# A decoder layer in fp32: one more pair of the down product in its 7-product form, four preparatory jobs moved ahead to the z products, a sixth pair's forms kept in device memory

## The chip, the cores and the metric

The kernel runs on one core of one Trainium2 chip. The metric is the device time of one execution in microseconds, the median of the runs. Before the change it is 992.4 us (three runs, 992.35 to 993.69).

## What is computed

One layer of a hybrid decoder: 256 tokens, 2048 features, float32. Cut to what matters here:

```python
h = rms_norm(x, g_mix)
z = h @ w_in                       # pool | q latent | kv latent | rope key | memory query
y = concat(pool_mixer(z_pool), mla(z_q, z_kv, z_kr), mem_attention(z_mq, mem))
x = x + y @ w_o
h = rms_norm(x, g_ffn)
g = causal_conv3(h @ w_gate) + conv_b
x = x + (silu(g) * (h @ w_up)) @ w_down      # 5632 hidden features
```

The change touches the last product, `@ w_down`, and when preparations for it are made.

## The kernel before, in words

**Arithmetic.** Every large product is made in three matmuls of a reduced float32 type: each operand is split into a high part (a rounding copy) and a low part (the rest), and high x high, low x high and high x low are added up in PSUM. For a weight tile, `split_w` has ScalarE write the high part `wh` (L102) and VectorE the low part `wl` (L103); there are four buffers of each, so the splits run at most four tiles of 128x1024 ahead of TensorE.

**Stages in order of time.** Memory keys and values (`mg`, until about 50 us); memory query and rope key (until 76.8); the z products, `gemm_z` (L140), six for the q and kv latents and one for the pool, with the memory attention between them (until about 126); pool, q and kv products with the rest of the attention preparation; output product `w_o` with the attention heads beside it; gate and up products, 44 steps f of two 1 MB weight tiles each (from about 302 to 770 us); down (770 to 987 us).

**Down.** The 5632 hidden features are 22 pairs of 128-wide blocks. A pair with the two halves of the tokens and the two 512-wide parts of 1024 columns makes a 2x2 block product. A plain pair (`plain`, L961) does its 8 block products, 3 matmuls each: 24 matmuls of 128x512. A pair in the 7-product form (`seven`, L990) does 7 products of sums of blocks (a Strassen-Winograd scheme): 21 matmuls. This needs sums of the activations' blocks, the "forms" `aS` (made in `glu` when the pair's gate and up steps are done, L892 to L900: 14 blocks of 128x128, 896 KB), and sums of the weight blocks (four subtractions of 128x512 on VectorE). Down runs over two halves c of the columns, and in each over the 22 pairs in the order `ORDER`. `KIND` gives the kind of each place in that order:

- p: plain; the pair's weight tile (1024 KB) is loaded and split;
- S: 7-product, with weight sums made earlier by a "job" and kept in device memory (`tsum`); in down three blocks of the weight tile (768 KB) and the tile of sums (1024 KB) are loaded;
- s: 7-product, with sums made in down by VectorE (`make_sums`, L982), which runs between the splits of the pair ahead.

Loads of down go out on SP's queue into six tiles in rotation (three `wr`, two `wj`, one in `dn`). Pairs in `AWAY` don't fit into SBUF: their forms are stored to device memory after `glu` (L902) and fetched again in each half into the one buffer `aL` (`fetch`, L975, on POOL's queue). The first fetch of a half is issued at its start, each further one right behind the pair that used the buffer (L1056).

**Jobs.** A job loads a weight tile of down (`job_load`, POOL's queue), makes its four sums in place on VectorE (`job_sums`, L760 to L766) and stores them to `tsum` in two pieces, again from POOL. Before, there are 30 jobs: eight during the output product (`first_jobs`), 22 during the gate and up products.

**What sets the order.** The code is recorded step by step; a scheduler may shift steps on an engine, except those marked `keep`, which stay in program order among themselves. Each engine then runs its list in order, and a DMA is issued when its queue reaches it and its waits are met. Job loads, job sums and stores are kept. The four buffers `wh` and `wl` and the load tiles are released by their last reader.

**Around the z products.** Three `wr` tiles hold the weights; SP loads them as they come free, with two loads of x rows (`x1n`, L538) among them. After the memory query, `mq_done` (L441) has ScalarE copy the results, TensorE transpose them and ScalarE write `mqT` (L282), which the memory scores (L511) use between the second z product's low and high parts.

Of the kernel before, what the change touches and what calls it, by code (L numbers as in the profile page):

```python
# [11 lines left out]
F32 = mybir.dt.float32  # L12
# [3 lines left out]
ALU = mybir.AluOpType  # L16
AX = mybir.AxisListType

P = 128
# [13 lines left out]
KF = DFF // P  # L33
# [3 lines left out]
STG = 2048  # L37
HS = 1024
NN = 512

PAIRS = KF // 2
KIND = "pSSSsSSpSSsSSSSsSSSSpp"
ORDER = (0, 1, 16, 2, 3, 4, 17, 5, 21, 6, 18, 7, 8, 9, 19, 10, 11, 12, 20, 13, 14, 15)
AWAY = (16, 17, 18, 19, 20)
SEVEN = tuple(j for j, k in zip(ORDER, KIND) if k != "p")
SUMMED = tuple((c, j) for c in range(2) for j, k in zip(ORDER, KIND) if k == "S")

# [17 lines left out]
def layer(ctx, tc, xT_d, xn_d, memT_d, vec_d, tab_d, w_z_d, w_mqkr_d, w_q_d, w_kv_d, w_mem_d, w_pool_d, w_o_d,  # L65
          w_g_d, w_u_d, w_dn_d, out_d):
    nc = tc.nc
# [8 lines left out]
    def nm(s):  # L76
        uid[0] += 1
        return f"{s}_{uid[0]}"

    def ps_main():  # L80
        return psm.tile([P, 512], F32, tag="m", name=nm("psm"))
# [4 lines left out]
    def load_w(src, n, cut=STG, kept=False):  # L86
        raw = stage.tile([P, STG], F32, tag="wr", name=nm("wr"), bufs=3)
        for c in range(0, n, cut):
            keep(nc.sync.dma_start(raw[:, c:min(n, c + cut)], src[:, c:min(n, c + cut)]), kept)
        return raw[:]  # L90

    def keep(ins, on=True):

        return tc.keep_in_program_order(ins) if on else ins
# [93 lines left out]
    def split_act(dst, src, scale=None, kept=False):  # L188


        h, l = (dst[:, 0], dst[:, 1]) if len(dst.shape) == 3 else (dst[:, 0:T], dst[:, T:2 * T])
        if scale is None:
            nc.scalar.copy(h, src)
            nc.vector.tensor_tensor(l, src, h.bitcast(F32), op=ALU.subtract)
        else:
            keep(nc.scalar.activation(h, src, AF.Copy, scale=scale), kept)
            keep(nc.vector.scalar_tensor_tensor(l, src, scale, h.bitcast(F32), op0=ALU.mult, op1=ALU.subtract), kept)
# [4 lines left out]
    def v(name, i=0):  # L202
        o = VOFF[name] + i
        return vec[:, o:o + 1]
# [9 lines left out]
    big = ctx.enter_context(tc.tile_pool(name="big", bufs=1))  # L214
    mix = ExitStack()
    mp = mix.enter_context(tc.tile_pool(name="mix", bufs=1))
# [18 lines left out]
    def tok():  # L235
        return mp.tile([P, 512], F32, tag="tok", name=nm("tok"), bufs=3)
# [105 lines left out]
    for c in range(KD // 2):  # L342
        raw = raw0 if c == 0 else load_w(w_mem_d[c], STG, HS if c == 1 else STG)
# [9 lines left out]
        if c % 2:  # L353
            h = slice(2 * c - 2, 2 * c + 2)
# [68 lines left out]
    for c in range(KD // 2):  # L423
        raw = load_w(w_mqkr_d[c], 2 * 576)
# [97 lines left out]
    def mem_steps(m):  # L522
        if m == 0:
            mq_done()
        for h, step in beside.get(m, ()):
            (mem_heads[h].score, mem_heads[h].turn, mem_heads[h].values)[step]()
        if m == 6:
            latent_scales()

    zl = mp.tile([P, 6, 2 * T], F32R, tag="zl", name="zl")  # L530
    zs = mp.tile([P, 2, T], F32, name="zs")

# [2 lines left out]
    for m in range(6):  # L535
        raw = load_w(w_z_d[m], STG)
        if m in (1, 3):
            keep(nc.sync.dma_start(x1n[:, m // 2, :], xn_d[m // 2]))  # L538
        ps = ps_main()[:, 0:T]
        gemm_z(ps, raw, xg, lambda: mem_steps(m), m % 2 == 1)  # L540
        a = zs[:, m // 4, :]
        if m % 4 == 0:
            nc.scalar.activation(a, ps, AF.Square)
        else:
            t = mp.tile([P, T], F32, tag="zsq", name=nm("zsq"), bufs=2)
            nc.scalar.activation(t[:], ps, AF.Square)
            nc.vector.tensor_tensor(a, a, t[:], op=ALU.add)
        split_act(zl[:, m, :], ps, v("g_q_lat", m) if m < 4 else v("g_kv_lat", m - 4))


    sl, sl2 = sm(4), sm(4)

    def latent_scales():
        ps = ps_aux()
        for i in range(2):
            col_sums(ps[:, 2 * i:2 * i + 2], zs[:, i, :])
        for i in range(2):
            o = slice(2 * i, 2 * i + 2)
            nc.vector.tensor_tensor(sl[:, o], ps[:, o], rx2, op=ALU.mult)
            rsqrt_(sl[:, o], sl[:, o], 1.0 / (QR if i == 0 else KVR))  # L560
            nc.vector.tensor_tensor(sl[:, o], sl[:, o], rx, op=ALU.mult)
        nc.vector.tensor_tensor(sl2, sl, sl, op=ALU.mult)
# [6 lines left out]
    def pool_in(g):  # L569
        raw = load_w(w_z_d[6 + g], STG)  # L570
        ps = ps_main()[:, 0:T]
        gemm_z(ps, raw, xg, lambda: mem_steps(6 + g), False) if g == 0 else gemm_t(ps, raw, 0, xg, range(KD))
        nc.vector.tensor_tensor(zp[:, g, :], ps, rxb[:], op=ALU.mult)
# [46 lines left out]
    def q_up(n):  # L620
        raw = load_w(w_q_d[n], STG)
        pss = [[ps_main()[:]] for _ in range(NT)]
        for i in range(2):
            hi, lo = split_w(raw, i * HS, HS)
            gemm_n(pss, hi.rearrange("p (k n) -> p k n", n=512), lo.rearrange("p (k n) -> p k n", n=512),
                   zl, 2 * i, i == 0, i == 1)
        for tt in range(NT):
            ps = pss[tt][0]
            t = tok()
            if n < 2:  # L630
                nc.scalar.copy(t[:], ps)
                head_sq(ssq_n[:, tt, 4 * n:4 * n + 4], t[:].rearrange("p (h d) -> p h d", d=NOPE))
                to_features(qnT[:, 4 * n:4 * n + 4], t, tt, 4, gqk[:, 0:1])
            else:
                t1 = tok()
                nc.scalar.copy(t1[:], ps)
                p3 = t1[:].rearrange("p (h d) -> p h d", d=ROPE)
                head_sq(ssq_r[:, tt, :], p3)
                rotate(t[:].rearrange("p (h d) -> p h d", d=ROPE), p3, 0, tt, H)
                to_features(qrT, t, tt, 4)  # L640
# [34 lines left out]


    pool_in(0)
    q_up(2)
    pool_in(1)
    kv_up(0)  # L680
# [65 lines left out]
        if done[0] == 4 * H + 4:  # L746
            mla_heads[H - 1].values()

    dp = ctx.enter_context(tc.tile_pool(name="dram", bufs=1, space=bass.MemoryType.DRAM))
    tsum = dp.tile([P, len(SUMMED), STG], F32, name="tsum")  # L750

    def job_place():
        return fp.tile([P, STG], F32, tag="wj", name=nm("wj"), bufs=2)[:]

    def job_load(i, raw):

        keep(nc.gpsimd.dma_start(raw, w_dn_d[SUMMED[i]]))
        return i, raw

    def job_sums(i, raw):  # L760

        r = raw.rearrange("p (b n) -> p b n", n=NN)
        for d, a, b in ((1, 0, 1), (0, 2, 0), (2, 2, 1), (3, 3, 2)):
            keep(nc.vector.tensor_tensor(r[:, d], r[:, a], r[:, b], op=ALU.subtract))  # L764
        for h in range(2):
            keep(nc.gpsimd.dma_start(tsum[:, i, h * HS:(h + 1) * HS], raw[:, h * HS:(h + 1) * HS]))  # L766

    FIRST = (1, 3, 4, 6, 7, 9, 10, 12)

    def first_load(i):  # L770
        return job_load(i, mp.tile([P, STG], F32, tag=("xgt", "zl")[i % 2], name=nm("wk"))[:])

    waiting = [first_load(i) for i in range(2)]
    parts = [0]

    def first_jobs():

        if parts[0] in FIRST:
            i, raw = waiting.pop(0)
            job_sums(i, raw)  # L780
            if i + 2 < len(FIRST):
                waiting.append(first_load(i + 2))
        parts[0] += 1

    def out_part(i, n, pss, c, o):
# [21 lines left out]
    for n, c in ((0, 1), (1, 1), (0, 0), (1, 0), (2, 0), (2, 1), (3, 0), (3, 1)):  # L807
        begun = n in pss
# [60 lines left out]
    def glu(f, psg, psu, home=None):  # L869
# [14 lines left out]
        if e == 0:  # L884
            aT[j] = (home if j == PAIRS - 1 else away() if j in AWAY
                     else fp.tile([P, 14, P], F32R, name=nm("aS"))[:])
# [6 lines left out]
        if e:  # L893
# [6 lines left out]
            nc.vector.tensor_tensor(lo, sf, hi.bitcast(F32), op=ALU.subtract)  # L900
            if j in AWAY:
                nc.gpsimd.dma_start(forms[:, AWAY.index(j)], aT[j])  # L902


    forms = dp.tile([P, len(AWAY), 14, P], F32R, name="forms")

# [11 lines left out]
            x1_rstd()  # L918
    mix.close()
    fp = ctx.enter_context(tc.tile_pool(name="ffn", bufs=1))  # L920
    job = job_load(len(FIRST), job_place())
    late = len(SUMMED) - len(FIRST)
    job_at = {1 + i * (KF - 7) // (late - 1): len(FIRST) + i for i in range(late)}
    for f in range(1, KF):
        rows = [load_w(w[f], STG, kept=True) for w in (w_g_d, w_u_d)]
        behind = (lambda p=pss: glu(0, *p)) if f == 1 else None
# [4 lines left out]
        if f in job_at:  # L931
            now, n = job, job_at[f] + 1
            job = job_load(n, job_place()) if n < len(SUMMED) else None
# [41 lines left out]
    def fetch(j):  # L975

        aT[j] = away()
        nc.gpsimd.dma_start(aT[j], forms[:, AWAY.index(j)])

# [57 lines left out]
    for c in range(2):  # L1037
        own_ps, com_ps = (ps_main, ps_aux) if c else (ps_aux, ps_main)
        own = {(t, n): own_ps()[:] for t in range(NT) for n in range(2)}
        com = None  # L1040
        rest = [j for j in ORDER if j in AWAY]
        fetch(rest.pop(0))
        for i, j in enumerate(ORDER):
            kept = c > 0 or i > 1
# [3 lines left out]
            elif i >= PAIRS - 2:  # L1048
                between = lambda s=i - PAIRS + 3: common(c, com, s)
            elif KIND[i + 1] == "s":  # L1050
                between = lambda j=ORDER[i + 1]: make_sums(c, j)
            if j in SEVEN:
# [95 lines left out]
```

## Time and profile before

| | |
|---|---|
| median of three runs | 992.4 us |
| profiled execution, its own time | 992.38 us |
| its span on the core | 990.6 us |
| TensorE busy in the span | 985.2 us (99%) |
| VectorE, ScalarE, POOL busy | 792.3, 579.9, 70.2 us |
| DMA moved | 300.67 MB, mean 304 GB/s |

In the profile, PE is TensorE's matmul and PEld its weight load, DVE VectorE, ACT ScalarE, SP the engine that only issues DMAs. A row of the timeline gives start, length, engine, line, operation, output <- inputs, and in brackets the idle time ahead with what ended it. A row of the waits view gives the sum of a wait, how often, and the longest. A row of a table by stretches gives from:to, its length, the busy time of PE, PEld, DVE, ACT and POOL with the number of instructions, then the granted clock, the DMA share and GB/s. A row of the DMA issues gives the transfer, the queue, how many, KB each and the median time from issue to landing. Matmuls overlap: one of 128x512 takes 0.39 us, but they follow each other every 0.227 us.

### The profile page before, as it was taken

The numbers are of one execution on the slowest core, as the hardware profiler recorded it, in microseconds if no ns is written. First come the engines' busy times: TensorE is split into PE (matmuls) and PEld (weight loads), VectorE is DVE, ScalarE is ACT, GpSimd is POOL, SyncE is SP. The second block draws the span as 40 slices with busy tenths as digits, with TensorE's granted clock in tenths as the row PEclk, the third lists the DMA queues.
The fourth block names the chain that finished last, engine by engine and source line by source line (L and its number), as shares of the span: only waits on it lengthen the run. The fifth ranks groups of instructions, "written<-read, shape, count | busy, mean of one in ns | idle before, by whom it ended". The sixth has DMA issues, their size and how long they took to land.

```text
span 990.6 us, 17344 instructions
## 1 busy us (share of the span) xinstructions
PE 985.2 (99%) x6864; PEld 911.7 (92%) x6864; DVE 792.3 (80%) x1189; ACT 579.9 (59%) x782; POOL 70.2 (7%) x136
## 2 busy tenths in 40 slices
PE   9999999999999999999999999999999999999998
PEld 8899988888889999999999999999999888888886
DVE  6868588888767787777878877777876889999997
ACT  6777665644566555545455445545554667857773
POOL 1100000011100000000100100110000000000000
PEclk9999999999999999999999999999999999999999
DMA  9867446679887978987897978889997999999993
GB/s 358 293 245 285 141 166 218 233 280 331 320 318 277 352 270 283 320 326 273 316 326 279 322 280 314 321 307 338 354 311 254 350 389 361 395 350 391 355 413 130
DMA packets 51732, 300.67 MB, mean 304 GB/s; under 512 B 5825, under 2 KB 6337, under 8 KB 25921
## 3 DMA queue, kind: packets, MB, share of 16 engines
q1 hardware_dynamic: 33984, 214.73, 59.5%
q0 software_dynamic: 17232, 84.03, 22.9%
q8 instruction: 54, 0.88, 0.3%
q10 hardware_dynamic: 432, 0.79, 0.2%
q14 instruction: 30, 0.24, 0.1%
HBM read 259.28 MB, written 40.24 MB: 302 GB/s over the span
## 4 chain that ended last, share of the span: by engine, by line
PE 98%; DVE 1%; DMA 0%; ACT 0%; issue 0%
PE psm L168 47%; PE psm L184 5%; PE psm L185 5%; PE psm L186 5%; PE psm L149 4%; PE psa L959 4%; PE psm L959 4%; PE psa L958 4%; PE psa L957 4%; PE psm L958 4%; PE psm L957 4%; PE psm L133 2%; PE psa L722 1%; PE psa L184 1%; PE psa L186 1%; PE psa L185 1%
## 5 line engine op out<-in xcount | busy, mean ns | idle before, releaser
L103 DVE TENSOR_TENSOR wl<-wr,wh 128x1024 fp32r<-128x1024 f32 (+2 forms) x346 | 399.2, 1163 | 126.2 <-ACT wh L102 109.2
L102 ACT CAST wh<-wr 128x1024 fp32r<-128x1024 f32 (+2 forms) x346 | 345.6, 1004 | 179.9 <-PE psm L168 83.6
L168 PE MATMUL psm<-h,wh 128*128 128x256 f32 x2752 | 319.3, 276 | 0.0
L168 PEld LDWEIGHTS psm<-h,wh 128*128 128x128 f32 x2752 | 315.4, 188 | 0.0
L168 PE MATMUL psm<-h,wl 128*128 128x256 f32 x1376 | 163.1, 276 | 0.0
L168 PEld LDWEIGHTS psm<-h,wl 128*128 128x128 f32 x1376 | 159.3, 188 | 0.0
L873 ACT ACTIVATE gc<-g,vec 128x256 f32<-128x256 f32 x44 | 26.5, 603 | 81.3 <-DVE g L871 80.3
L103 DVE TENSOR_TENSOR wl<-wj,wh 128x1024 fp32r<-128x1024 f32 (+1 forms) x50 | 53.8, 1092 | 9.0 <-ACT wh L102 5.4
L764 DVE TENSOR_TENSOR wj<-wj 128x512 f32<-128x512 f32 x88 | 60.3, 685 | 0.8
L102 ACT CAST wh<-wj 128x1024 fp32r<-128x1024 f32 (+1 forms) x50 | 47.5, 949 | 19.2 <-PE psm L958 11.5
L876 ACT ACTIVATE gc<-gc 128x256 f32<-128x256 f32 x44 | 18.4, 418 | 55.6 <-DVE gc L875 55.6
L875 DVE SCALAR_TENSOR_TENSOR gc<-g,vec,gc 128x255 f32<-128x255 f32 x88 | 42.2, 480 | 1.5
L102 ACT CAST wh<-dn 128x1024 fp32r<-128x1024 f32 (+1 forms) x36 | 35.8, 994 | 9.8 <-PE psa L958 4.1
L103 DVE TENSOR_TENSOR wl<-dn,wh 128x1024 fp32r<-128x1024 f32 (+1 forms) x36 | 40.3, 1146 | 1.5 <-ACT wh L102 0.4
L766 POOL DMA_DIRECT2D tsum<-wj x44 | 23.5, 534 | 209.8 <-DVE s L896 93.9
L184 PE MATMUL psm<-wh,cat 128*128 128x512 f32 x96 | 38.1, 397 | 0.0
L186 PE MATMUL psm<-wl,cat 128*128 128x512 f32 x96 | 37.4, 390 | 0.0
L185 PE MATMUL psm<-wh,cat 128*128 128x512 f32 x96 | 37.4, 389 | 0.0
L957 PE MATMUL psm<-wh,aS 128*128 128x512 f32 x91 | 35.4, 390 | 0.0
L957 PE MATMUL psa<-wh,aS 128*128 128x512 f32 x91 | 35.4, 390 | 0.0
L958 PE MATMUL psm<-wh,aS 128*128 128x512 f32 x91 | 35.4, 389 | 0.0
L958 PE MATMUL psa<-wh,aS 128*128 128x512 f32 x91 | 35.4, 389 | 0.0
(253 smaller groups left out, 1473.4 us busy)
## 6 DMA issues: line engine op xcount, KB each, us to landing
wr<-in_w_g SPq DMA_DIRECT2D x44, 1024.0 KB, 7.0
wr<-in_w_u SPq DMA_DIRECT2D x44, 1024.0 KB, 7.1
wj<-in_w_dn POOLq DMA_DIRECT2D x22, 1024.0 KB, 7.8
tsum<-wj POOLq DMA_DIRECT2D x44, 512.0 KB, 6.9
wr<-in_w_o SPq DMA_DIRECT2D x16, 1024.0 KB, 6.2
wr<-tsum SPq DMA_DIRECT2D x15, 1024.0 KB, 7.4
wr<-in_w_dn SPq DMA_DIRECT2D x16, 768.0 KB, 6.9
wr<-in_w_z SPq DMA_DIRECT2D x10, 1024.0 KB, 6.9
```

The source lines that it names most:

```text
L102: keep(nc.scalar.copy(hi[:, c:e], raw[:, o + c:o + e]), kept)
L103: keep(nc.vector.tensor_tensor(lo[:, c:e], raw[:, o + c:o + e], hi[:, c:e].bitcast(F32), op=ALU.subtract), kept)
L149: keep(nc.tensor.matmul(ps, parts[k // nk][low][:, i * P:(i + 1) * P], m, start=k + a == 0 and low == low_first, stop=k == KD - 1 and low ...
L168: nc.tensor.matmul(ps, parts[k // nk][low][:, i * P:(i + 1) * P], m, start=k + a == 0 and low == (s == 1), stop=k == KD - 1 and low == (s ...
L184: keep(nc.tensor.matmul(ps, xh, hi[:, i, o], start=first and i == 0, stop=False), kept)
L185: keep(nc.tensor.matmul(ps, xl, hi[:, i, o], start=False, stop=False), kept)
L186: keep(nc.tensor.matmul(ps, xh, lo[:, i, o], start=False, stop=last and i == nk - 1), kept)
L764: keep(nc.vector.tensor_tensor(r[:, d], r[:, a], r[:, b], op=ALU.subtract))
L875: nc.vector.scalar_tensor_tensor(gc[:, d:T], g[:, 0:T - d], v(w, f), gc[:, d:T], op0=ALU.mult, op1=ALU.add)
L957: nc.tensor.matmul(ps, a[0], b[0], start=first, stop=False)
L958: nc.tensor.matmul(ps, a[1], b[0], start=False, stop=False)
L959: nc.tensor.matmul(ps, a[0], b[1], start=False, stop=last)
```

## The change

Three tables are new (places are counted from 0): the pair at place 7 goes from p to S, that at place 15 from s to S, and the pairs kept away are six instead of five. They stand at places 2, 5, 9, 12, 15 and 18 instead of 2, 6, 10, 14 and 18. So there are 19 7-product pairs instead of 18, 17 of them with jobs (34 jobs instead of 30) and two instead of three with sums made in down.

```diff
-KIND = "pSSSsSSpSSsSSSSsSSSSpp"
-ORDER = (0, 1, 16, 2, 3, 4, 17, 5, 21, 6, 18, 7, 8, 9, 19, 10, 11, 12, 20, 13, 14, 15)
-AWAY = (16, 17, 18, 19, 20)
+KIND = "pSSSsSSSSSsSSSSSSSSSpp"
+ORDER = (0, 1, 15, 2, 3, 16, 4, 5, 21, 17, 6, 7, 18, 8, 9, 19, 10, 11, 20, 12, 13, 14)
+AWAY = (15, 16, 17, 18, 19, 20)
...
+    MID = 4
+    wa = big.tile([P, 3, STG], F32, tag="act", name="wa")
+    wb = big.tile([P, STG], F32, tag="act2", name="wb")
+    mid = []
+
+    def mid_jobs(m):
+
+        if m in (2, 3):
+            for i in (2 * m - 4, 2 * m - 3):
+                mid.append(job_load(i, wa[:, i, :] if i < 3 else wb[:]))
+        if m > 2:
+            job_sums(*mid.pop(0))
...
         split_act(zl[:, m, :], ps, v("g_q_lat", m) if m < 4 else v("g_kv_lat", m - 4))
+        mid_jobs(m)
...
     pool_in(0)
+    mid_jobs(6)
     q_up(2)
```

The first four jobs use the room of the tiles `act` and `act2` between the memory stage's `mg` and the queries' and keys' tile `qkv`. `job_load` and `job_sums` themselves are only moved up in the file. The eight jobs of the output product and the 22 of the gate and up products keep their places, with the numbers of the jobs shifted by four.

On POOL, before the change, these are the last loads ahead of the output product's first jobs (x and s are rows of the input, wk the jobs' tiles; the memset clears a part of `qkv`):

```order
L356 DMA x_81<-in_xT 128x1024 x3
L603 MEMSET qkv 128x2048
L405 DMA s_64_565<-in_xn 128x1024
L356 DMA x_81<-in_xT 128x1024
L405 DMA s_73_623<-in_xn 128x1024
L405 DMA s_79_661<-in_xn 128x1024
L405 DMA s_85_699<-in_xn 128x1024
L757 DMA wk_2019<-in_w_dn 128x2048
L757 DMA wk_2021<-in_w_dn 128x2048
```

and after it:

```order
L405 DMA s_85_699<-in_xn 128x1024
L538 DMA wa<-in_w_dn 128x2048 x3
L538 DMA wb<-in_w_dn 128x2048
L547 DMA tsum<-wa 128x1024 x6
L636 MEMSET qkv 128x2048
L547 DMA tsum<-wb 128x1024 x2
L538 DMA wk_2049<-in_w_dn 128x2048
L538 DMA wk_2051<-in_w_dn 128x2048
```

The four loads stand directly behind the last load of x rows, with nothing of the z products between; the memset has moved behind the stores of three jobs.

On VectorE, behind the fourth z product, before the change (wl are low parts of weights, zs and zl belong to the latents, catm, st and p to the memory attention):

```order
L103 TENSOR_TENSOR wl_1291<-wr_1287,wh_1290 128x1024
L547 TENSOR_TENSOR zs<-zs,zsq_1195 128x256
L197 SCALAR_TENSOR_TENSOR zl<-psm_1113,vec,zl 128x256
L103 TENSOR_TENSOR wl_1295<-wr_1287,wh_1294 128x1024
L194 TENSOR_TENSOR catm<-psa_1243,catm 128x256
L481 TENSOR_REDUCE st_1252<-psa_1248 128x1 x2
L482 TENSOR_TENSOR st_1252<-st_1252,small 128x2
```

and after it:

```order
L103 TENSOR_TENSOR wl_1312<-wr_1308,wh_1311 128x1024
L579 TENSOR_TENSOR zs<-zs,zsq_1202 128x256
L197 SCALAR_TENSOR_TENSOR zl<-psm_1120,vec,zl 128x256
L545 TENSOR_TENSOR wa<-wa 128x512
L103 TENSOR_TENSOR wl_1316<-wr_1308,wh_1315 128x1024
L545 TENSOR_TENSOR wa<-wa 128x512 x3
L194 TENSOR_TENSOR catm<-psa_1258,catm 128x256
L481 TENSOR_REDUCE st_1267<-psa_1263 128x1 x2
```

A job's four subtractions stand around a split; the three other jobs come in the same way, one z product later each.

On TensorE in down, before the change, the end of the first pair that uses `aL` and the start of the next one (rows 1669 and 1733 of its list; aS are forms that stay in SBUF):

```order
L958 MATMUL psa_8931<-wh_9030,aL_8933 128x512
L959 MATMUL psa_8931<-wl_9031,aL_8933 128x512
L957 MATMUL psm_8969<-wh_9060,aS_3699 128x512
...
L959 MATMUL psa_8931<-wl_9157,aS_4235 128x512
L957 MATMUL psm_8969<-wh_9184,aL_9055 128x512
L958 MATMUL psm_8969<-wh_9184,aL_9055 128x512
```

and after it (rows 1669 and 1712):

```order
L974 MATMUL psa_8965<-wh_9064,aL_8967 128x512
L975 MATMUL psa_8965<-wl_9065,aL_8967 128x512
L973 MATMUL psm_9003<-wh_9094,aS_3729 128x512
...
L975 MATMUL psa_8965<-wl_9150,aS_3997 128x512
L973 MATMUL psm_9003<-wh_9178,aL_9089 128x512
L974 MATMUL psm_9003<-wh_9178,aL_9089 128x512
```

Between the two uses of the buffer there were 63 matmuls, three pairs, and now there are 42, two pairs. The same holds at places 9 to 12, 12 to 15 and 15 to 18; from 5 to 9 it is three pairs.

More of the change, by code (lines that the diff above doesn't have):

```diff
@@ L528, in mem_steps, with job_place, job_load, job_sums @@
             latent_scales()
+    dp = ctx.enter_context(tc.tile_pool(name="dram", bufs=1, space=bass.MemoryType.DRAM))
+    tsum = dp.tile([P, len(SUMMED), STG], F32, name="tsum")
+    def job_place():
+        return fp.tile([P, STG], F32, tag="wj", name=nm("wj"), bufs=2)[:]
+    def job_load(i, raw):
+        keep(nc.gpsimd.dma_start(raw, w_dn_d[SUMMED[i]]))
+        return i, raw
+    def job_sums(i, raw):
+        r = raw.rearrange("p (b n) -> p b n", n=NN)
+        for d, a, b in ((1, 0, 1), (0, 2, 0), (2, 2, 1), (3, 3, 2)):
+            keep(nc.vector.tensor_tensor(r[:, d], r[:, a], r[:, b], op=ALU.subtract))
+        for h in range(2):
+            keep(nc.gpsimd.dma_start(tsum[:, i, h * HS:(h + 1) * HS], raw[:, h * HS:(h + 1) * HS]))
+    MID = 4
[8 more added lines that the diff above has]
+            job_sums(*mid.pop(0))
     zl = mp.tile([P, 6, 2 * T], F32R, tag="zl", name="zl")
@@ L747, in mla_steps @@
             mla_heads[H - 1].values()
[L749 to L766, printed above, removed]
     FIRST = (1, 3, 4, 6, 7, 9, 10, 12)
     def first_load(i):
-        return job_load(i, mp.tile([P, STG], F32, tag=("xgt", "zl")[i % 2], name=nm("wk"))[:])
+        return job_load(MID + i, mp.tile([P, STG], F32, tag=("xgt", "zl")[i % 2], name=nm("wk"))[:])
     waiting = [first_load(i) for i in range(2)]
@@ L780, in first_jobs @@
             job_sums(i, raw)
-            if i + 2 < len(FIRST):
-                waiting.append(first_load(i + 2))
+            if i + 2 < MID + len(FIRST):
+                waiting.append(first_load(i + 2 - MID))
         parts[0] += 1
@@ L920, in layer @@
     fp = ctx.enter_context(tc.tile_pool(name="ffn", bufs=1))
-    job = job_load(len(FIRST), job_place())
-    late = len(SUMMED) - len(FIRST)
-    job_at = {1 + i * (KF - 7) // (late - 1): len(FIRST) + i for i in range(late)}
+    begun = MID + len(FIRST)
+    job = job_load(begun, job_place())
+    late = len(SUMMED) - begun
+    job_at = {1 + i * (KF - 7) // (late - 1): begun + i for i in range(late)}
     for f in range(1, KF):
```

## The prediction

> **What bounds the kernel now.** I read the page first, for the engine that is never idle, then the chain of waits.
>
> ```profile
> span 990.6 us, 17344 instructions
> PE 985.2 (99%) x6864; PEld 911.7 (92%) x6864; DVE 792.3 (80%) x1189; ACT 579.9 (59%) x782; POOL 70.2 (7%) x136
> PE 98%; DVE 1%; DMA 0%; ACT 0%; issue 0%
> ```
>
> TensorE is busy for 985.2 of 990.6 us and carries 98% of the chain. So the time is the number of matmuls times their spacing, plus whatever makes TensorE wait. The profiled execution took 992.38 us, 1.8 us more than its span, and the median of the three runs is 992.4: I add all terms to 992.4. About 0.2% (2.0 us) is what a measurement of this kernel can tell from no change.
>
> Next I read the table by stretches, since the change adds transfers in two places: the stage of the z products (62 to 130 us) and down (770 to 987 us).
>
> ```profile
> 62.00:82.00 20.00, 20.00 (x156) 19.95 (x156) 11.49 (x22) 12.81 (x25) 0.00 (x0) 1.00 0.92 352
> 74.00:78.00 4.00, 4.00 (x33) 4.00 (x33) 2.30 (x3) 1.44 (x2) 0.00 (x0) 1.00 1.02 412
> 90.00:126.00 36.00, 36.00 (x295) 35.22 (x295) 22.32 (x44) 24.80 (x47) 0.00 (x0) 1.00 0.44 157
> 126.00:136.00 10.00, 10.00 (x65) 9.04 (x65) 7.16 (x16) 5.27 (x8) 0.00 (x0) 1.00 0.33 115
> 136.00:160.00 24.00, 23.66 (x154) 20.65 (x153) 23.30 (x48) 15.42 (x27) 0.00 (x0) 1.00 0.52 176
> 770.00:970.00 200.00, 200.00 (x877) 163.34 (x876) 181.98 (x192) 142.25 (x154) 6.98 (x13) 1.00 0.98 377
> 834.00:870.00 36.00, 36.00 (x159) 29.47 (x158) 33.38 (x36) 27.30 (x30) 1.06 (x2) 1.00 1.01 403
> ```
>
> The last two columns are the DMA share and GB/s. When the share is full the engines move 403 to 412 GB/s; between 90 and 136 us they are half idle; from 62 to 82 us, and all through down, they are nearly full. The granted clock is 1.00 throughout.
>
> **Part 1: one more pair in the 7-product form.** A plain pair of down takes 24 matmuls in each half of the columns, a 7-product pair 21. TensorE's rows at the start of the first plain pair and of the two 7-product pairs after it price both:
>
> ```profile
> 769.88 0.40 PE L957 MATMUL psa<-wh,aT 128*128 128x512 f32 x1
> 775.35 0.39 PE L957 MATMUL psm<-wh,aS 128*128 128x512 f32 x1
> 780.11 0.39 PE L957 MATMUL psm<-wh,aL 128*128 128x512 f32 x1
> ```
>
> That is 5.47 us against 4.76, or 0.227 us for each matmul. The pair at place 7 loses three matmuls in each half: 6 x 0.227 = **-1.4 us**, all of it on the path.
>
> **Part 2: one pair fewer whose sums VectorE makes in down.** In front of such a pair (an "s" in the table) the matmuls of a low part come late:
>
> ```profile
> 787.59 0.39 PE L958 MATMUL psm<-wh,aS 128*128 128x512 f32 x1
> 787.82 0.39 PE L957 MATMUL psm<-wh,aS 128*128 128x512 f32 x1
> 788.16 0.73 PE L959 MATMUL psm<-wl,aS 128*128 128x512 f32 x2
> 788.73 0.39 PE L958 MATMUL psm<-wh,aS 128*128 128x512 f32 x1
> 788.96 0.40 PE L957 MATMUL psa<-wh,aS 128*128 128x512 f32 x1
> ```
>
> Five steps take 1.37 us instead of 1.135, so an "s" costs 0.23 us. Three in each half become two: **-0.5 us** in all. The plain pair at place 7 gave VectorE a rest which is lost, but its next "s" (place 10) now comes six pairs after the first, so I price this loss at nothing; without that cover it costs at most another 0.23 us in each half, 0.5 us.
>
> **Part 3: the forms of six pairs are fetched, every three pairs instead of every four.** There is one buffer for them (`aL`). Its next fetch waits on POOL until TensorE has done the last matmul with the old contents, and must land before the next pair of this kind begins. These are such a last matmul, the fetch that it releases, the landing times of the nine fetches in down, and the first of them by itself with its weight load:
>
> ```profile
> 803.97 0.39 PE L959 MATMUL psa<-wl,aL 128*128 128x512 f32 x1
> 804.67 0.54 POOL L978 DMA_DIRECT2D aL<-forms  x1 [18.54 <-PE psa L959]
> DMA to landing us min/median/max: 7.7/9.4/10.1
> aL<-forms POOLq DMA_DIRECT2D x1, 896.0 KB, 9.6
> L957 PEld LDWEIGHTS psm<-wh,aL 128*128 128x128 f32 x35 | 6.6, 188 | 1.4
> ```
>
> The fetch starts 0.7 us after that matmul started. Today three or more pairs lie between; after the change, two 7-product pairs lie between at four of the five gaps of a half. From the last old matmul to the first new one are then 43 steps of 0.227, 9.76 us. Less the 0.7 ahead of the fetch and 0.27 for its wake-up and the weight load of 0.188, 8.8 us are left for landing. The median fetch needs 9.4, so TensorE waits 0.6 us. In two of the four gaps an "s" wait of 0.23 already stretches the window, so 0.4 there. Both halves: 4 x 0.6 + 4 x 0.4 = **+4.0 us**. Bounds: no wait if all land like the best (7.7), 8 x 1.3 = 10.4 us if all like the worst (10.1). I take the median since these fetches met the same loads as they will. Only the out_t stores between the halves stand behind a fetch on POOL's queue, and TensorE alone waits for it.
>
> Down also moves more: in each half a tile of sums twice where there was none (768 + 1024 KB in place of 1024 KB at two places, 2 x 0.786 MB) and one fetch of 0.918 MB: 2.5 MB, or 5.0 MB in all, 12.4 us of a full DMA at 403 GB/s. Room from 770 to 970 us: 200 x (403 - 377) = 5.2 MB, most of it outside the stretches where the last pairs of a half are loaded. Today no split on ScalarE waits for a load in down; its first waits are all for TensorE:
>
> ```profile
> ACT wh L102 <- PE psa L958: 29.0, 51, 3.7
> ACT wh L102 <- PE psm L958: 24.0, 48, 1.7
> ACT wh L102 <- DVE wl L103: 3.4, 12, 0.3
> ```
>
> The fetch waits slow TensorE by 2 us in each half and so give loads room; I add **+0.5 us** for late loads, between 0 (all room is used) and 12.4 (none is).
>
> **Part 4: four jobs beside the z products.** In the code the loads stand at the third and fourth z product. In POOL's order nothing stands ahead of them but the last load of x rows, and they wait for the memory stage alone, long over. So they are issued from 61.9 us on, straight into the fullest stretch:
>
> ```profile
> 61.38 0.53 POOL L405 DMA_DIRECT2D s<-in_xn  x1 [2.23 <-ACT s L410]
> wr<-in_w_z SPq DMA_DIRECT2D x1, 1024.0 KB, 4.8
> ACT wh L102 <- DMA wr<-in_w_z: 4.3, 2, 2.6
> 71.92 4.67 SPq L89 DMA_DIRECT2D wr<-in_w_z  x2
> wr<-in_w_z SPq DMA_DIRECT2D x1, 1024.0 KB, 10.3
> 82.30 2.00 ACT L102 CAST wh<-wr 128x1024 fp32r<-128x1024 f32 x2
> 84.20 1.26 ACT L282 ACTIVATE mqT<-psa,small 128x512 f32<-128x512 f32 x2
> 85.43 1.89 PE L511 MATMUL psa<-mkT,mqT 128*128 128x256 f32 x8
> ```
>
> Alone, a z load lands after 4.8 us (the one at 107.7): 2.5 of transfer and 2.3 fixed. The z load issued at 71.92 takes 10.3, lands at 82.2, and ScalarE splits it at once. Behind that split in ScalarE's queue stand the two copies into mqT, and TensorE's scores need them at 85.43, with no slack of more than 0.3 us. So what delays this landing delays TensorE.
>
> The jobs bring 4 x 1.049 = 4.2 MB. By the fetch row of part 3, POOL's transfers beside a busy SP queue get 0.918 MB in 9.4 - 2.3 = 7.1 us, 129 GB/s, 31% of 412. From 64.2 (61.9 and the fixed part) to 82.2 that is 2.3 MB. Free room there is 20 x (412 - 352) = 1.2 MB. The rest, 1.1 MB, delays the landing by 2.7 us, and as the jobs go on taking 31% meanwhile, by 2.7 / 0.69 = 3.9. Less the 0.3: **+3.6 us**. Bounds: 0 if the room is used wholly by the jobs, and all their data ahead of that load, (4.2 - 1.2) / 0.412 = 7.3, less 0.3, 7.0.
>
> Their sums are 16 subtractions on VectorE, by this row 11.0 us:
>
> ```profile
> L764 DVE TENSOR_TENSOR wj<-wj 128x512 f32<-128x512 f32 x88 | 60.3, 685 | 0.8
> ```
>
> From 90 to 136 us VectorE is free for 16.5 of 46 us, which covers them. The last job comes after the seventh z product, just ahead of 136 to 160, where VectorE is busy for 23.3 of 24 and TensorE already misses 0.3. I add **+0.5**, between 0 and one job, 2.7. The stores of these sums, 4.2 MB, fall where the DMA is half idle: nothing; without that cover 10 us of DMA. POOL's memset of the queries' tile now waits for those stores; its first reader, and the next loads on POOL, come behind all the pool, q and kv products: nothing, unless it slips past those.
>
> The sixth store of forms and the extra sums of one pair lie in the gate and up products, where PE shows no gap and VectorE has a fifth of its time free: nothing; at most one split, 1.1 us.
>
> **Sum:** 992.4 - 1.4 - 0.5 + 4.0 + 0.5 + 3.6 + 0.5 = **999.1 us**.
>
> **Rivals.**
> A. The two queues share evenly. Then a fetch gets 206 GB/s, lands after 2.3 + 4.5 = 6.8 us, under 8.8, and costs nothing; the jobs take half in the z stage, which reaches the bound of 7.0. 992.4 - 1.9 + 7.0 + 0.5 + 0.5 = 998.5. Against it: no fetch landed under 7.7. The Trainium skill ("DMA: Bandwidth & Descriptors", section "Queues, rings and completion order") says just this, that each DMA engine takes turns between the queues that have work, a packet at a time; the fetch row's 31% disagrees with equal turns, and the measurement decides. Chance 0.10.
> B. The z loads hold: the jobs only fill room. Decides if the load issued at 71.9 lands by 82.5. 992.4 - 1.9 + 4.5 + 0.5 = 995.5. For it: the share of 62 to 82 is 0.92, not 1. Chance 0.08.
> C. The fetches land in time, the z stage waits: 992.4 - 1.9 + 3.6 + 0.5 = 994.6. Chance 0.05.
> D. Down becomes bound by DMA: all 12.4 us come out, as the room can't be used ahead of time with six tiles of buffer. 992.4 - 1.9 + 12.4 + 4.1 = 1007.0. For it: 403 GB/s at full share. Against it: ScalarE never waits for a load there. Chance 0.06.
> E. Faster: TensorE's count alone decides. It holds if every fetch lands within 8.8 us, as the best of the nine (7.7) did, and the z load by 82.5: 990.5, and 990.0 if VectorE is also less late at the second "s". Chance 0.09, about half of it beyond 0.2%.
>
> **How the numbers follow.** My forecast has 0.62. The range leaves out D, E and little else: low 994.5 (best fetches, B or C), high 1006.0 (the z stage at 7, the fetches at 8, late loads at 0.5). Faster by over 0.2%, 0.04 (half of E); within 0.2% (990.4 to 994.4), 0.08 (the other half of E, and C's lower end); slower, 0.88.
>
> **What would show it.** Right: the waits view names TensorE's weight loads of `aL` waiting for the DMA, some 0.5 us each at places 5, 12, 15 and 18; gaps of TensorE of 3 to 4 us in sum between 70 and 88 us, with ScalarE waiting for z loads that land after more than 11 us; down some 2.5 us longer than today. Wrong: fetches under 8.8 us, z loads landing as before, or ScalarE in down waiting for loads first.

## The result, and the profile after

The changed kernel takes **1005.8 us** (median of four runs, 1004.73 to 1007.67) against 992.66 us before, timed beside it (four runs, 992.35 to 993.69): a ratio of 1.0134, interval 1.0122 to 1.0146. The profiled execution took 1005.98 us. The page:

```profile
span 1004.0 us, 17405 instructions
PE 987.4 (98%) x6858; PEld 912.3 (91%) x6858; DVE 804.0 (80%) x1204; ACT 583.5 (58%) x785; POOL 78.2 (8%) x151
```

The span grew by 13.4 us although TensorE has six matmuls (1.4 us) fewer, so it waits or runs slowly for 14.8 us more; its idle time alone went from 5.4 to 16.6 us. Four points on its rows tell where. Each is the start of a matmul: the first of gate and up, the first of down, the last of down; then the end of the span.

| | before, us | after, us | added in this stage |
|---|---|---|---|
| gate and up begin | 301.67 | 309.21 | **+7.5** |
| down begins | 769.88 | 777.42 | 0.0 |
| last matmul begins | 986.32 | 997.56 | **+3.7** |
| span ends | 990.6 | 1004.0 | **+2.2** |

Those are the rows of down's first and last matmul:

```profile
777.42 0.40 PE L973 MATMUL psa<-wh,aT 128*128 128x512 f32 x1
...
997.56 0.39 PE L975 MATMUL psm<-wl,aT 128*128 128x512 f32 x1
```

The table by stretches, for the z stage and down:

```profile
62.00:82.00 20.00, 17.89 (x133) 17.18 (x132) 7.78 (x11) 8.05 (x13) 1.86 (x4) 1.00 0.97 386
84.00:90.00 6.00, 4.33 (x21) 3.62 (x22) 5.52 (x19) 4.76 (x14) 0.00 (x0) 0.78 1.01 421
88.00:90.00 2.00, 2.00 (x12) 2.00 (x11) 1.97 (x10) 0.76 (x3) 0.00 (x0) 0.50 0.99 414
777.00:977.00 200.00, 195.37 (x857) 159.31 (x856) 178.47 (x185) 141.40 (x153) 8.04 (x15) 1.00 1.00 390
```

From 62 to 88 us TensorE has holes, and behind them its granted clock falls: 0.78 over 84 to 90 us, 0.50 in the last two of them, where it was 1.00 throughout before. In down it is idle for 4.6 of 200 us. TensorE's waits, of which the largest lie in just these two stages:

```profile
PE psa L973 <- DMA aL<-forms: 2.1, 2, 1.1
PE psa L278 <- ACT tok L446: 1.9, 2, 1.4
PE psm L973 <- DMA aL<-forms: 1.5, 2, 1.0
PE psm L149 <- ACT wh L102: 1.3, 1, 1.3
...
PE psm L975 <- DVE wl L103: 1.0, 1, 1.0
PE psa L184 <- ACT wh L102: 0.5, 1, 0.5
```

**The z stage.** The queues' shares (packets, MB, share of the DMA engines; q0 is POOL's queue, q1 that of SP) and the issues from 62 to 82 us, and the shares from 72 to 84 us, where both queues have work all the time:

```profile
q0 software_dynamic: 648, 4.26, 53.4%
q1 hardware_dynamic: 595, 3.44, 43.1%
...
wr<-in_w_z SPq DMA_DIRECT2D x4, 1024.0 KB, 13.2
wa<-in_w_dn POOLq DMA_DIRECT2D x3, 1024.0 KB, 14.0
```

```profile
q1 hardware_dynamic: 348, 2.58, 51.2%
q0 software_dynamic: 345, 2.51, 49.9%
```

POOL's queue got not 31% but more than half: 4.26 MB in 20 us, 213 GB/s. SP's queue had moved 6.5 MB in the same stretch before. All four jobs were in at 86.22 us, ahead of the z load whose landing the prediction watched. That load reaches ScalarE's split, and behind it the copies into mqT, here:

```profile
89.49 2.00 ACT L102 CAST wh<-wr 128x1024 fp32r<-128x1024 f32 x2 [1.24 <-DMA wr<-in_w_z]
91.39 1.26 ACT L282 ACTIVATE mqT<-psa,small 128x512 f32<-128x512 f32 x2
```

Both were at 82.30 and 84.20, so they come 7.19 us later. Half of this, 3.6 us, is a later issue of the load (75.52 instead of 71.92, since its tile comes free later), the other half a longer way (13.9 us to landing instead of 10.3).

The wait that was foreseen, that of the scores for mqT, is nevertheless not in the waits view: TensorE comes late to the scores by itself. These are its rows before (the scores began at 85.43) and after:

```profile
76.76 3.87 PE L149 MATMUL psm<-xg,wh 128*128 128x256 f32 x32
80.46 1.04 PE L278 MATMUL psa<-identf,tok 128*128 128x128 f32 x8
81.58 4.01 PE L149 MATMUL psm<-xg,wl 128*128 128x256 f32 x32
```

```profile
79.42 4.04 PE L149 MATMUL psm<-xg,wh 128*128 128x256 f32 x32 [1.35 <-ACT wh L102]
84.88 0.69 PE L278 MATMUL psa<-identf,tok 128*128 128x128 f32 x4 [1.42 <-ACT tok L446]
...
87.46 5.57 PE L149 MATMUL psm<-xg,wl 128*128 128x256 f32 x32
92.87 0.38 PE L511 MATMUL psa<-mkT,mqT 128*128 128x256 f32 x1
```

The first z product begins 2.7 us late: the loads of the memory query and of this product land late. The transposes begin 4.4 late: the next z load is late too, and the copies of the memory query (L446) stand behind its split on ScalarE. The low part of the first z product begins 5.9 late and takes 5.57 us instead of 4.01, at the lower clock. That makes 7.4 at the scores, the whole loss of the stage but 0.1. Without the lower clock the scores would have met the foreseen wait: they began 1.23 us after the copies into mqT before, and that would be 92.62, only 0.25 earlier (an estimate from these rows).

**Down.** The fetches in down landed after 8.6 to 10.5 us, and the pairs at places 12 and 15 of the first half and 12 and 18 of the second began 0.7 to 1.2 us late. This is the worst of the first half:

```profile
851.85 0.39 PE L975 MATMUL psa<-wl,aS 128*128 128x512 f32 x1
853.25 0.47 PE L973 MATMUL psm<-wh,aL 128*128 128x512 f32 x1 [1.01 <-DMA aL<-forms]
```

The wait is 1.01 us, and with the weight load the step from matmul to matmul grows from 0.23 to 1.40. The four steps together, less 0.227 each, are 4.3 us, and 4.7 with the step behind each, which takes 0.31. One load that came late in front of an "s" adds 1.0 (the L975 row of the waits): VectorE waits for it with its sums for 0.9 us, and the split that TensorE needs stands behind them.

**The end.** From the start of the last matmul to the end of the span it is now 6.4 us, before 4.3. Nothing in the prediction spoke of that. The experiments take it up.

### The profile page after: what moved, and what is told of

It is laid out like the page before. It is cut to its first block, busy times and chain, and to the rows that moved or that the text cites. A ratio compares the mean times of both kernels' runs of the same rounds, so it can differ in the third digit from the quotient of the medians.

```text
span 1004.0 us, 17405 instructions
## 1 busy us (share of the span) xinstructions
PE 987.4 (98%) x6858; PEld 912.3 (91%) x6858; DVE 804.0 (80%) x1204; ACT 583.5 (58%) x785; POOL 78.2 (8%) x151
## 5 line engine op out<-in xcount | busy, mean ns | idle before, releaser
L103 DVE TENSOR_TENSOR wl<-wr,wh 128x1024 fp32r<-128x1024 f32 (+2 forms) x350 | 404.5, 1163 | 129.7 <-ACT wh L102 112.9
L103 DVE TENSOR_TENSOR wl<-wj,wh 128x1024 fp32r<-128x1024 f32 (+1 forms) x52 | 56.4, 1099 | 7.5 <-ACT wh L102 3.1
L103 DVE TENSOR_TENSOR wl<-dn,wh 128x1024 fp32r<-128x1024 f32 (+1 forms) x34 | 37.6, 1127 | 5.0 <-ACT wh L102 4.5
L102 ACT CAST wh<-dn 128x1024 fp32r<-128x1024 f32 (+1 forms) x34 | 32.9, 978 | 14.8 <-PE psm L974 7.4
```

The costliest lines, as they stand in the source:

```text
L102: keep(nc.scalar.copy(hi[:, c:e], raw[:, o + c:o + e]), kept)
L103: keep(nc.vector.tensor_tensor(lo[:, c:e], raw[:, o + c:o + e], hi[:, c:e].bitcast(F32), op=ALU.subtract), kept)
```

## The experiments

Before and after are as above; the stage times below are read as in the table. Single runs stand beside 992.5 to 992.7 us for the kernel before on the same chip.

### 1. The four loads late, on SP's queue

```diff
-    def job_load(i, raw):
+    def job_load(i, raw, eng=nc.gpsimd):
...
-        keep(nc.gpsimd.dma_start(raw, w_dn_d[SUMMED[i]]))
+        keep(eng.dma_start(raw, w_dn_d[SUMMED[i]]))
...
-        if m in (2, 3):
-            for i in (2 * m - 4, 2 * m - 3):
-                mid.append(job_load(i, wa[:, i, :] if i < 3 else wb[:]))
...
         raw = load_w(w_z_d[m], STG)
+        if m in (3, 4):
+            for i in (2 * m - 6, 2 * m - 5):
+                mid.append(job_load(i, wa[:, i, :] if i < 3 else wb[:], nc.sync))
```

> The four early jobs keep their sums and stores, but their loads stand on SP's queue behind the loads of the fourth and fifth z product instead of on POOL's at 61.8 us. Theory (the z stage lost 7.5 us because four 1 MB loads on POOL's queue took every second turn from 61.8 to 86.2 us, just when z0 to z2 were fetched): the start of gate and up comes back from 309.2 to 302 to 303.5 us, total 998.5 to 1000. Rival 1 (VectorE's 16 subtractions and the memset of krT, which waits for the jobs, hold the stage): gate and up still start after 307, total 1004 to 1006. Rival 2 (the loads cost wherever they stand in this stage, since four loads and four stores need 20 us of DMA in it): the start lies at 305 to 308, total 1002 to 1004.

996.02 us. Gate and up begin at 302.31, 0.6 later than before. The stretch and ScalarE's copies stand as they did before the change:

```profile
62.00:82.00 20.00, 20.00 (x157) 19.95 (x156) 12.81 (x24) 14.12 (x28) 0.00 (x0) 1.00 0.93 356
...
82.86 1.26 ACT L282 ACTIVATE mqT<-psa,small 128x512 f32<-128x512 f32 x2
```

So the sums, the stores and the memset cost 0.6 us at most; the time at which the loads run, or the queue that they are on, costs 7 us. The total fell by some 3 us more than these 7, below what was expected: down and the end were 1.3 us shorter each, with the same code there.

### 2. The sums of the four jobs left out

```diff
-    def job_sums(i, raw):
+    def job_sums(i, raw, sums=True):
...
-        for d, a, b in ((1, 0, 1), (0, 2, 0), (2, 2, 1), (3, 3, 2)):
+        for d, a, b in ((1, 0, 1), (0, 2, 0), (2, 2, 1), (3, 3, 2)) if sums else ():
...
-            job_sums(*mid.pop(0))
+            job_sums(*mid.pop(0), sums=False)
```

> The four early jobs load and store as after the change, but their 16 subtractions on VectorE are left out, so that tsum holds plain weights for them and the output of these pairs is not the layer's. Theory (loads in POOL's queue): the z stage stays 6.5 to 8 us late, gate and up start at 308 to 310, total 1005 to 1006. Rival (VectorE's sums delay the splits and with them TensorE): the start comes back by 2 us or more, to 307 or less, total 1003 or less.

1008.59 us, and gate and up begin at 312.28: not VectorE. It got worse than either theory said, and the queues tell why. Without the sums the stores no longer wait; three pairs of them go out at 72.6, 77.7 and 82.4 us, on POOL's queue too, which so keeps its turns for longer. The copies into mqT slip to 93.34, and now TensorE's scores do wait for them:

```profile
PE psa L511 <- ACT mqT L282: 3.1, 1, 3.1
```

From 88 to 104 us only these stores are left on POOL's queue, and they show what is shared:

```profile
q1 hardware_dynamic: 615, 4.51, 66.8%
q0 software_dynamic: 618, 2.25, 34.7%
```

Both queues move the same number of packets, but those of the stores are of 4 KB and those of the loads of 8 KB. The turns are equal in packets, so a queue's share of the bytes goes by the size of its packets.

### 3. The four loads late, but on POOL's queue

```diff
-        if m in (2, 3):
-            for i in (2 * m - 4, 2 * m - 3):
-                mid.append(job_load(i, wa[:, i, :] if i < 3 else wb[:]))
+        if m in (1, 2):
+            for i in (2 * m - 2, 2 * m - 1):
+                raw = wa[:, i, :] if i < 3 else wb[:]
+                keep(nc.vector.memset(raw[:, 0:1], 0.0))
+                mid.append(job_load(i, raw))
```

> The four early loads stay on POOL's queue, but each waits for a one-column write of its tile by VectorE behind the second and the third z product, some 25 us later than after the change; everything else as after the change. Theory (the time at which they run costs, since z0 to z2 are then not yet in, and not the queue): the start of gate and up comes back to 302 to 303.5 us, total 996 to 999. Rival (a load on POOL's queue takes every second turn from the z loads wherever it stands, and only SP's own queue avoids that): start at 305 or later, total over 1000.

999.29 us; gate and up begin at 301.84, 0.2 later than before. The loads went out at 93.3 and 99.5 us, and from 85 to 115 us POOL's queue had 40.8% of the DMA engines beside 46.3% for SP's, and it hurt nobody. (This is a mean over 30 us in which now one queue and now the other was nearly alone, and no measure of their turns.) So it is the time: late, the loads cost 0.6 us at most on either queue. The total is 0.3 above what was expected, by fetch waits of 5.0 us in down.

### 4. No job in the z stage

The four jobs run beside gate and up instead (26 there instead of 22).

```diff
-    MID = 4
...
+    MID = 0
     mid = []
 
     def mid_jobs(m):
 
-        if m in (2, 3):
-            for i in (2 * m - 4, 2 * m - 3):
-                mid.append(job_load(i, wa[:, i, :] if i < 3 else wb[:]))
-        if m > 2:
-            job_sums(*mid.pop(0))
+        pass
```

> No job runs in the z stage; all 34 but the eight of the output product run beside gate and up (26 instead of 22), tables of the change kept. Theory (gate and up are bound by TensorE, VectorE 78% busy, DMA share 0.86, and four more jobs go between): gate and up start at 301.5 to 302, last 468 to 469 us, total 996 to 999 (down as after the change, with its fetch waits). Rival (gate and up have no room left for four jobs): the stage takes 471 us or more, total over 1000.

998.99 us. Gate and up begin at 301.81, which leaves the z stage whole, and last 469.55 us instead of 468.21, a little over the 468 to 469 expected; in experiment 8, with the same jobs, they last 468.21. Gate and up have room for four more.

### 5. The pairs kept away set further apart

```diff
-ORDER = (0, 1, 15, 2, 3, 16, 4, 5, 21, 17, 6, 7, 18, 8, 9, 19, 10, 11, 20, 12, 13, 14)
+ORDER = (0, 15, 1, 2, 3, 16, 4, 5, 21, 17, 6, 7, 18, 8, 9, 10, 19, 11, 12, 20, 13, 14)
```

> The six pairs kept away stand at places 1, 5, 9, 12, 16 and 19, so that only two gaps per half are three places wide instead of four; all else as after the change. Theory (a fetch takes 8.6 to 10.5 us, and a window of two pairs gives it 8.8): half of the 4.5 us of fetch waits goes, and place 1 waits for nothing since its fetch is issued when the buffer comes free; down lasts 2 to 3 us less (first to last matmul 217.1 to 218.1 instead of 220.1), total 1003 to 1004. Rival (down is limited by its transfers, and TensorE meets the next late load instead): down lasts 219.5 to 220.5, total 1005.5 to 1006.

1003.91 us; first to last matmul of down 218.0 us, 2.1 less. Places 1, 5 and 16 wait for nothing; 12 in both halves and 19 in the second still do. With gaps of four places a fetch has its time, with three it mostly has not.

### 6. A second buffer for the fetched forms

```diff
-    def away():
-        return fp.tile([P, 14, P], F32R, tag="aL", name=nm("aL"), bufs=1)[:]
+    def away(n=0):
+        return fp.tile([P, 14, P], F32R, tag=("aL", "s8")[n % 2], name=nm("aL"), bufs=1)[:]
...
-        aT[j] = away()
+        aT[j] = away(AWAY.index(j))
...
-                if j in AWAY and rest:
+                if (j in AWAY or i == 1) and rest:
```

> A second buffer for fetched forms (laid over the tile of the sums of gate and up, which is idle in down), so that each fetch is issued one away pair earlier; the second fetch of a half behind place 1; all else as after the change. Theory (4.5 us of down are waits for fetches that have too short a window): no wait for aL is left, down lasts 215.5 to 217 us instead of 220.1, total 1001 to 1002.5. Rival (down is bound by its transfers; what the fetches no longer wait for, the loads do): down lasts 218.5 or more, total 1004 or more.

1000.87 us. Down takes 214.5 us from first to last matmul, better than both: 5.6 less than after, 1.9 less than before. No wait for aL is left in the waits view. The stretch of down:

```profile
778.00:978.00 200.00, 200.00 (x880) 163.99 (x879) 182.82 (x188) 145.34 (x158) 8.00 (x15) 1.00 1.01 401
```

The DMA share is 1.01, so the engines are full, and TensorE has no gap. The rival, that loads come late instead, falls: in this run a full share was not yet a bound, with each fetch issued earlier. The fetches land after 7.6 to 9.9 us (median 9.0), hardly faster than with one buffer (8.6 to 10.5, median 9.3).

### 7. The end: program order for the last pair

In the changed kernel the scheduler put four low matmuls (L975) of the last pair together near its end, so that the first of VectorE's final steps (L1047) could begin 4.5 us after the pair's start; before it was 3.6. This run keeps that pair's matmuls bank after bank.

```diff
-        nc.tensor.matmul(ps, a[0], b[0], start=first, stop=False)
+        keep(nc.tensor.matmul(ps, a[0], b[0], start=first, stop=False), kept)
...
```

> The matmuls of the last pair of each half are kept in program order, bank after bank, so that the four low matmuls no longer stand together near the end; all else as after the change. Theory (the 2.2 us lost behind the last matmul come from the order: the first finish could start 4.5 us after the pair's start instead of 3.6): the first three finishes run beside the matmuls, last matmul start to end of span falls from 6.4 to 4.3 to 5.0 us, TensorE waits up to 0.8 us more for wl, total 1004.5 to 1005.5. Rival (it is the landing of the last output store, 3.1 us instead of 2.1): the stretch stays at 5.8 to 6.5 us, total 1005.8 to 1006.8.

1009.21 us: slower, against both. The end itself shortened as the theory said, to 4.8 us, but ahead of it TensorE lost 4.0. Its rows in the last pair, and two stretches behind the wait:

```profile
993.42 0.39 PE L974 MATMUL psm<-wh,aT 128*128 128x512 f32 x1
995.96 0.50 PE L975 MATMUL psm<-wl,aT 128*128 128x512 f32 x1 [2.15 <-DVE wl L103]
...
997.51 0.63 PE L974 MATMUL psm<-wh,aT 128*128 128x512 f32 x1
997.94 0.63 PE L975 MATMUL psm<-wl,aT 128*128 128x512 f32 x1
```

```profile
995.90:1001.00 5.10, 5.04 (x15) 4.04 (x16) 1.67 (x4) 0.00 (x0) 0.00 (x0) 0.67 0.27 103
997.00:1000.00 3.00, 3.00 (x8) 2.34 (x7) 1.00 (x2) 0.00 (x0) 0.00 (x0) 0.50 0.23 87
```

The low part of the second half of the last weights (wl) is made behind VectorE's common step, 3.4 us after the pair's start. The scheduler's order had hidden that; mine made TensorE wait 2.15 us, and soon after this wait matmuls followed each other every 0.43 us instead of 0.227, at a granted clock of 0.50 from 997 to 1000 us. I had allowed 0.8 us for the wait and nothing for the clock. The cure is to move the split ahead of the common step, and not the matmuls; the next runs have it.

### 8. Jobs in gate and up, two buffers, the split ahead

Experiments 4 and 6 together, and in the last pair of each half:

```diff
-        if between is not None:
+        if between is not None and not by_bank:
             between()
         ws.append(split_w(raw, HS, HS, kept=kept))
+        if by_bank:
+            between()
```

> Jobs in gate and up, two buffers for fetched forms, and in the last pair of each half the split of the second half of the weights put ahead of the common step on VectorE; tables of the change kept. If the three terms (z stage 7.5, fetch waits 4.5, order at the end 0.8) are the whole of the loss, the total is 990.5 to 993, level with or up to 2 us under the time before. Rival (a new wait, late loads of down or VectorE in gate and up, takes their place): 994 to 998.

992.02 us (eleven runs, 991.24 to 996.82) beside 992.50: ratio 1.000, interval 0.999 to 1.001. So the three terms account for the loss, but for the end. Down is 1.65 us shorter than before, z stage and gate and up are level, and the end is 1.0 longer, 0.8 of it by the landing of the last store.

### 9. Loads late on SP, two buffers, the split ahead

> The job loads late on SP's queue (as in the first experiment), two buffers for fetched forms, and the last pair's second split ahead of the common step. From the parts: span of the first experiment 994.2, less its fetch waits of 3.9 in down beyond the usual half us, less 0.9 by the order at the end: 989 to 990.5, total 990.8 to 992.3. The last store: in all kernels so far in which an instruction fetch of 8 KB runs on one DMA engine between its issue and its landing it takes 2.4 to 3.4 us, and 2.1 to 2.2 in the two where none does. If that is the cause, 2.1 to 2.3 here where no such fetch lies there, as in the first experiment, and 2.8 or more where one does; a rival (it varies by itself) has no such tie.

991.03 us (eleven runs) beside 992.72: **ratio 0.9984, interval 0.9975 to 0.9993**, 1.7 us faster than before and so faster than both kernels. Down takes 214.14 us from first to last matmul, 2.3 less than before; gate and up begin at 302.85, 1.2 later than before, and last 0.3 less. TensorE waits for no DMA and no split any more; the whole waits view:

```profile
PE psa L318 <- DVE ones L222: 1.1, 1, 1.1
PE psa L494 <- DVE p L488: 0.3, 1, 0.3
PE psa L278 <- DVE small L212: 0.2, 1, 0.2
PE psa L278 <- DVE tok L651: 0.2, 1, 0.2
```

And the end is 4.2 us, 0.1 shorter than before. The last store and what else the DMA engines did from its issue on, first in the changed kernel (999.6 to 1002.9 us), then here (986 to 988.3):

```profile
q1 hardware_dynamic: 353, 0.62, 51.2%
q14 instruction: 1, 0.01, 2.0%
...
out_t<-dn SPq DMA_DIRECT2D x1, 256.0 KB, 3.1
```

```profile
q1 hardware_dynamic: 294, 0.52, 60.1%
...
out_t<-dn SPq DMA_DIRECT2D x1, 256.0 KB, 2.0
```

In the first, one packet of instructions runs in that window: 2.0% of sixteen engines in 3.3 us is one engine for 1.06 us. The trace of the changed kernel shows what it holds up. The packet starts at 1000.76 us and takes 1.05, until 1001.81. The store closes with sixteen packets of 4 bytes; fifteen of them start at 1001.21 to 1001.36, the last at 1002.45, behind eight packets of 2 KB that follow each other from 1001.81 on, when nothing else is left of the store. It fits in every profile here: eight kernels with such a packet between the last store's issue and its landing took 2.4 to 3.4 us for it, the kernel before and experiments 1, 9 and 10 without one 2.0 to 2.2. No run moved the packet alone.

### 10. No sums in down at all

Experiment 8 with jobs for the two "s" pairs too: 38 jobs, 30 of them beside gate and up.

```diff
-KIND = "pSSSsSSSSSsSSSSSSSSSpp"
+KIND = "pSSSSSSSSSSSSSSSSSSSpp"
```

> Jobs in gate and up, two buffers, the last pair's split ahead, and also jobs for the two pairs whose sums VectorE makes in down (38 jobs, 30 of them in gate and up; these pairs then load 1792 KB instead of 1024 KB). If VectorE's sums are what holds these places (0.24 and 0.4 us each, in both halves) and gate and up take four more jobs: down 1.0 to 1.3 us shorter than 214.8, total 990.5 to 992. Rival (down's DMA, at a share of 0.92, has no room for 3 MB more): loads come late at the end of the halves, down 216 or more, total over 993.

1016.78 us, ratio 1.0244, interval 1.0221 to 1.0266. In down the rival held: the two "s" waits are gone, but late loads cost TensorE 2.8 us at places 17 and 18 (1.1 in the first half, 1.8 in the second), and down takes 216.5, at a DMA share of 1.02 over 794 to 994 us. But 24 us are lost where neither looked, in gate and up (492 us). VectorE's and TensorE's waits there:

```profile
DVE wj L545 <- DMA wj<-in_w_dn: 21.2, 8, 7.0
```

```profile
PE psm L168 <- DVE wl L103: 15.0, 8, 7.9
```

A job keeps one of the two tiles `wj` through load, sums and stores. With 30 jobs in 37 steps the load of the next is not in when VectorE reaches its sums, and the splits that TensorE needs stand behind them in VectorE's queue. With 22 jobs (after) and 26 (experiments 4 and 8) VectorE waits there for the load of a job for 0.3 us in all at most.

## Why the prediction was wrong, point by point

Direction and places were right, the size was not: it moved by 13.1 us where 6.7 were forecast. That this is still just inside the range is luck: its upper end allowed 7.0 for the z stage and 8 for the fetches (with the 0.5 for VectorE these terms give 1006.5, not 1006.0), and what filled it was 7.5 in the z stage, about 4.5 for the fetches and 2.2 at the end, which no term stood for.

- **Matmuls and one "s" fewer (-1.4 and -0.5): right.** Experiments 6, 8 and 9, with no fetch wait left, have down 1.9, 1.7 and 2.3 us under before.
- **Fetch waits (+4.0): right in the mechanism and the sum.** 4.3 to 4.7 us in the profile of after; 2.7 to 5.0 by the waits view in the runs with one buffer and these gaps. The spread is not the forecast one: eight waits of 0.4 to 0.6 were expected, and four came, of 0.7 to 1.2, none of them at place 5. The late loads (+0.5) were 1.0 in that profile and 0.7 in experiment 5; experiments 4 and 7 have one late split of 0.9 each, whose cause was not followed, and 1 to 3 have none. Both together, by what the second buffer took away, 5.6 against 4.5.
- **The loads in the z stage (+3.6): the step that failed.** The z loads were held up by the jobs, as described, and the watched one came 7.2 us late instead of 3.9. The wait came one link earlier than described: the scores waited for nothing, since late splits of the loads ahead, and the lower clock behind those waits (1.6 us, with no term in the sum), had held TensorE up for as long already. The step that failed is the rate: "POOL's transfers beside a busy SP queue get 0.918 MB in 9.4 - 2.3 = 7.1 us, 129 GB/s, 31%". A landing time less a start-up time is not a share. This is that fetch of before (issued at 785.6, landed at 795.2), cut in three by queue, at 785 to 788.8, 789 to 792 and 792 to 795.2 us:

```profile
q1 hardware_dynamic: 213, 1.41, 101.9%
```

```profile
q0 software_dynamic: 127, 0.84, 77.9%
q1 hardware_dynamic: 49, 0.28, 30.6%
```

```profile
q1 hardware_dynamic: 174, 1.22, 91.7%
q0 software_dynamic: 16, 0.07, 5.9%
```

It moves nothing for 3 us, then nearly all at 280 GB/s, then has a thin tail. There never was a rate of 129. The other eight fetches of before look alike: the first packet comes 2.5 to 3.8 us after the issue (a z load alone on SP's queue has it after 1.0), the middle 80% of the bytes take 2.0 to 3.4 us, which is 214 to 365 GB/s, and the last packets run until 7.4 to 9.6 us after the issue. So the 2.3 taken off for the start was a z load's, and the tail was counted as transfer. With four loads standing in POOL's queue there is no pause between them (none over 0.3 us from 62.5 to 85 us), and the queue held its half of the packets. The rival A gave for this the bound of 7.0, and 7.5 was measured. I rejected A by a row that measured latency.

The Trainium skill ("DMA: Bandwidth & Descriptors", section "Queues, rings and completion order") says that each DMA engine takes turns between the queues that have work, a packet at a time. The trace agrees: 345 packets beside 348 from 72 to 84 us, and 618 beside 615 in experiment 2, with half the bytes for the queue with the smaller packets.

Where A failed is the other half: it took a fetch for 6.8 us by the same turns, and fetches took 8.6 to 10.5 us all the same. Start-up and tail, not the share, make a single fetch long.
- **The sums on VectorE (+0.5): nothing.** In experiment 3 all sixteen are there and gate and up begin 0.03 us later than in experiment 4, which has none.
- **Nothing for the end: missed, 2.2 us.** I priced down to its last matmul and took what follows as fixed. 0.8 of it is the last pair's new order: the first final step begins 4.5 instead of 3.6 us after the pair's start, while the four steps together take 2.7 against 2.8. 1.0 is the last store's landing. The other 0.3 lies around them and was not looked into. The change leaves both places untouched in the code; a scheduler's order and the place of an instruction fetch changed with the rest.
- **Rival D (bound by DMA in down): wrong, for a reason worth keeping.** The share did go to 1.00, but experiments 6 and 9 run at 1.01 without a wait. With the 3 MB more of experiment 10 late loads did cost time, at 1.02, so the room was nearly used up.

## What to carry to other kernels

Before a transfer is moved to another queue, ask when its queue will reach it, not where it stands in the code: with nothing to wait for, it starts at once, and beside a busy queue it takes half of the packets here. The same four loads cost 7 us at 62 us and 0.2 at 93. And price a queue's share from the bytes that it moves while it is busy (a table by queue in a narrow window), not from issue to landing.

## What the runs showed of the hardware

- A wait of TensorE of 2.15 us was followed by matmuls every 0.43 us instead of 0.227 for some 3.4 us (granted clock 0.50 from 997 to 1000, experiment 7): the wait itself was only half of the 4.0 us that it cost. In the z stage of after, the clock fell to 0.50 (88 to 90 us) behind several gaps of 0.3 to 1.4 us, and 32 matmuls took 1.6 us longer. Four waits of 0.5 to 1.1 us far apart in down left it at 1.00.
- Two busy DMA queues moved equal numbers of packets, so the queue with packets of 4 KB got half the bytes of the one with 8 KB (2.25 and 4.51 MB, experiment 2).
- One instruction fetch of 8 KB ran for 1.05 us beside the last store, and eight pieces of that store followed only when it ended: the store landed after 3.1 us instead of 2.1. That both were on one DMA engine is read from these times; the trace does not name the engine.
